# Stick breaking: the first head's weights kept, both heads' value products in one run

## The chip, the cores and the metric

The kernel runs on one core of one Trainium2 chip. The metric is the device time of one execution in microseconds (us), the median of several runs. The engines that matter here are TensorE (PE in the rows, and PEld for its weight loads), VectorE (DVE), ScalarE (ACT), GpSimd (POOL) and SyncE (SP), which issues the DMAs. Each works through its own instructions in the order in which they stand in the built program, and waits on semaphores for the others.

## The reference, cut to what matters

A trunk of two layers (512 tokens, width 1024). Each layer runs five attention branches with four heads of 64 dimensions from one projection, gates and merges them, and projects back. The change lies in the stick-breaking branch:

```
z = einsum('bqhd,bshd->bhqs', q_blk, k) * scale
strict = s_pos[None, :] < t[:, None]
log_keep = where(strict, log_sigmoid(-z), 0.0)
later = cumsum(log_keep, axis=3, reverse=True) - log_keep
a = where(strict, exp(log_sigmoid(z) + later), 0.0)
y = einsum('bhqs,bshd->bqhd', a, v)
```

## The kernel before, in words

One program, written with a tile layer that allocates buffers from pools, sets all semaphores, and decides the order of instructions on each engine by priority (in the main the order of the code) and by when buffers and inputs come free. Weights are streamed from HBM by SP in pieces of 128x1024 (`wraw`, L278); ACT rounds each piece to a high part (`whi`, L269), DVE subtracts to get the low part (`wlo`, L270), and PE multiplies in three terms, high by high, high by low and low by high (`pj`, all recorded at L259, the line of the helper `mm`). These `pj` products are most of the program. `weave` mixes generators in fixed ratios, so that an attention branch, whose steps wait for one another, stands between projections.

`sb_attn(pr)` (L921) does the stick breaking of head pair `pr`: heads 2pr (e=0) and 2pr+1 (e=1). It works on transposed scores: keys in blocks of 128 (j=3, 2, 1, 0) on the partitions, queries in the columns. Since only later queries see a key block, block j has 512-128j columns: 128, 256, 384 and 512. For each block `begin` puts the scores into a PSUM bank `sbz` (tags S and T) and computes softplus on ACT and DVE (`sp_t`), `store` splits it into a high and a low part (`sp`), `middle` adds the sums over later keys by products of `sp` with constant matrices (`ntri`, `nones`) and takes the exponential (`sb_a`, from the pool tag PT with four buffers), and `end` multiplies with the values: output `Yc`, 64 partitions (the lower half for e=0, the upper for e=1), weights `VC` of 64 columns, moving tile `sb_a`, both plain float32, which the trace records as two instructions for each product. The blocks are pipelined over three steps, so `end` of a block stands two blocks behind its `begin`. After the eighth `end`, L988 multiplies with the gate and splits the result. The stages are `weave((sb_attn(0), 8), ...)` at L1363 and L1367 and `weave((sb_attn(1), 8), ...)` at L1370, in both layers.

Other attention branches multiply with the values in `pv_pair` (L558, output `Y`): also 64 columns of weights, blocks of 128 columns, with the heads in turns, e=1, e=0.

Buffers of 128x512 float32 for nearly everything else come from the pool `st` with `NST` slots: stacked queries and keys of each branch, loads of small tables (`cbt`, L877) and of the compression weights (`wc`, L1077), temporaries. `fox_proj` (L1186) makes its sixteen stacked tiles while `dsa_attn` (L1042) still holds twelve of queries and keys and two of values.

Of the kernel before, what the change touches and what calls it, by code (L numbers as in the profile page):

```python
# [10 lines left out]
F32 = mybir.dt.float32  # L11
# [10 lines left out]
T = 512  # L22
# [3 lines left out]
EPS = 1e-6  # L26
NEG = -1e30
REPL = -3e38
NST = 31

IN_LAYOUT = (
    ('dsa_q', 256), ('dsa_ckv', 128), ('idx_q', 128), ('idx_k', 32), ('idx_w', 4), ('dsa_z', 256),
# [154 lines left out]
def trunk(ctx: ExitStack, tc: tile.TileContext, xt, memt, pos, wall, small, vec, ca, cb, out):  # L187
# [3 lines left out]
    def after(ins, *earlier):  # L191
        for e in earlier:
            if e is not None:
                tc.add_manual_dep(ins.ins, e.ins.name, dep_info, reason="issue order")
# [6 lines left out]
    wts = pool("wts")  # L201
    st = pool("st", bufs=NST)
    wk = pool("wk")
# [7 lines left out]
    def bank(name, tag, shape=(128, 512)):  # L211
        return ps.tile(list(shape), F32, name=name, tag=tag, bufs={"pj": 3, "S": 2, "T": 3}[tag])
# [45 lines left out]
    def mm(out_, lhsT, rhs, start, stop, **kw):  # L258
        return nc.tensor.matmul(out_, lhsT, rhs, start=start, stop=stop, **kw)  # L259
# [297 lines left out]

    def pv_pair(Y, pr, V, PTs, nblk, last):  # L558

        after_qk = recent[-1]  # L560
        for j in range(nblk):
            for e in (1, 0):
                m = mm(Y[64 * e:64 * e + 64, pr], V(e, j), PTs[e][:, 128 * j:128 * j + 128], j == 0, j == nblk - 1)
                after(m, last, after_qk)
# [3 lines left out]
    def causal(blocks, lag):  # L568

        pend = []  # L570
        for i, scores, sums, mask, V, done in blocks:
            n = 128 * (i + 1)
            st_ = {"Y": None, "last": None, "PT": []}
            for h in range(4):
# [4 lines left out]
                def finish(i=i, h=h, P=P, V=V, done=done, st_=st_):  # L579
# [6 lines left out]
                    if h == 3:  # L586
                        done(st_["Y"])

# [87 lines left out]
    def layer(l, xs, begin):  # L676
        vo = l * V_L
        lv = SimpleNamespace(begin=begin)
# [242 lines left out]
        def sb_attn(pr):  # L921
            SPW = [512, 384, 256, 256]
            if pr == 0:
                sp = big.tile([128, 6, T], F32R, name="sp", tag="xa")
                lv.SP = [[sp[:, 2 * min(j, 2) + s, 256 * (j == 3):256 * (j == 3) + SPW[j]] for s in range(2)] for j in range(4)]
                for s in range(2):
                    nc.vector.memset(f32(lv.SP[3][s][:, 0:128]), 0.0)
            SP = lv.SP
            out = {}

            def begin(e, j):

                h = 2 * pr + e
                n, w = SPW[j], T - 128 * j
                ks = slice(128 * j, 128 * j + 128)
                z = bank("sbz", "S" if j % 2 else "T")[:, :n]
                mm(z, lv.KC[h][:, ks], lv.QC[h][:, T - n:], True, False)
                mm(z, lv.KlC[h][:, ks], lv.QC[h][:, T - n:], False, False)
                mw = n - w + 128
                mm(z[:, :mw], identb, sbm[:, 256 - mw:], False, True)  # L940
                zw = z[:, n - w:]
                t = wk.tile([128, T], F32, name="sp_t", tag="P", bufs=3)[:, :w]
                nc.scalar.activation(t, zw, AF.Abs)
                lnexp(t, t, AF.Exp, scale=-1.0)
                lnexp(t, t, AF.Ln, bias=ones1)
                nc.vector.scalar_tensor_tensor(t, zw, 0.0, t, op0=OP.max, op1=OP.add)
                return e, j, z, t

            def middle(e, j, z, t):

                n = SPW[j]
                for jj in range(3, j - 1, -1):
                    for s in range(2):
                        mm(z[:, n - SPW[jj]:], ntri if jj == j else nones, SP[jj][s], False, jj == j and s == 1, skip_group_check=True)
                w = T - 128 * j
                a = wk.tile([128, T], F32, name="sb_a", tag="PT", bufs=4)[:, :w]
                lnexp(a, z[:, n - w:], AF.Exp)
                return e, j, a

            def store(e, j, z, t):  # L960
                shi, slo = (x[:, SPW[j] - (T - 128 * j):] for x in SP[j])
                nc.vector.tensor_copy(shi, t)
                nc.vector.tensor_sub(slo, t, f32(shi))

            def end(e, j, a):
                h = 2 * pr + e
                if not out:
                    out["Y"] = bank("Yc", "T")
                mm(out["Y"][64 * e:64 * e + 64, 128 * j:], lv.VC[:, j, 64 * h:64 * h + 64], a, j == 3, j == 0, skip_group_check=True)

            one = two = None
            for e in range(2):
                for j in (3, 2, 1, 0):
                    new = begin(e, j)
                    nxt = middle(*one) if one else None
                    store(*new)
                    if two:
                        end(*two)
                    one, two = new, nxt
                    yield  # L980
            if two:
                end(*two)
            end(*middle(*one))
            Y = out["Y"]
            if pr == 0:
                lv.YC = y_tiles()
            y = slot("yC")
            nc.vector.tensor_mul(y, Y, lv.ZC[0][:, pr])  # L988
            split(y, lv.YC[0][:, pr], lv.YC[1][:, pr])
# [424 lines left out]
```

## Time and profile before

| | |
|---|---|
| runs | 1373.56, 1374.56, 5024.1 us, median 1374.56 |
| profiled execution | 1373.34 us; span from the first to the last instruction 1371.6 us |
| PE busy | 1340.4 us, 98% of the span |
| DVE busy | 894.6 us, 65% |
| ACT busy | 691.2 us, 50% |
| DMA | 124.12 MB, mean 90 GB/s |
| mean granted TensorE clock | 0.997 |

Busy time is the union of an engine's instructions; PE's matmuls overlap their neighbours, so what one costs is read from the distance between the starts of instructions. 1.74 us of the profiled execution lie outside its span.

### The profile page before, as it was taken

To read this page: it belongs to the slowest core of one execution; us is meant where nothing else is said; L and a number is where in the kernel's file an instruction comes from. 1 tells how busy PE (TensorE), PEld (TensorE's weight loads), DVE (VectorE), ACT (ScalarE), POOL (GpSimd) and SP (SyncE) were. 2 spreads that over 40 slices of the span, in tenths; PEclk is the share of its full clock that TensorE was granted. 3 is DMA by queue.
4 is the path that set the end of the run, shared out by engine and by line. 5 is a ranking of instruction groups with operands and counts; after the bars stand their busy time and mean duration, and the time that the engine had idled before them with its cause. 6 is when DMAs were issued, how large, how long until landed. Compare 5 with 4: busy or idle time off the path is not lost. (4 is left out here: it accounts for less than half of the span.)

```text
span 1371.6 us, 19089 instructions
## 1 busy us (share of the span) xinstructions
PE 1340.4 (98%) x7240; PEld 1078.3 (79%) x7240; DVE 894.6 (65%) x1869; ACT 691.2 (50%) x1322; POOL 11.0 (1%) x28
## 2 busy tenths in 40 slices
PE   7999999999999999999999999999999999999997
PEld 6777787877788788888886777778777878887897
DVE  6877999756655444545567599995675463455454
ACT  6877825356545434434347586443574453343330
POOL 0000000000000000000000000000000000000000
PEclk9999999999999999999999999999999999999999
DMA  6441232222112222124524213212212222223231
GB/s 218 131 139 56 68 102 83 84 70 73 62 62 99 71 92 76 61 92 133 179 76 137 79 62 112 75 61 93 62 62 77 70 92 70 92 77 106 90 112 62
DMA packets 40236, 124.12 MB, mean 90 GB/s; under 512 B 4432, under 2 KB 6480, under 8 KB 40144
## 3 DMA queue, kind: packets, MB, share of 16 engines
q1 hardware_dynamic: 40144, 122.89, 27.9%
q8 instruction: 57, 0.93, 0.3%
q14 instruction: 35, 0.29, 0.1%
HBM read 118.16 MB, written 4.72 MB: 90 GB/s over the span
## 5 line engine op out<-in xcount | busy, mean ns | idle before, releaser
L259 PE MATMUL pj<-h_hi,whi 128*128 128x512 f32 x1088 | 431.9, 398 | 0.0
L259 PE MATMUL pj<-h_lo,whi 128*128 128x512 f32 x1088 | 429.2, 395 | 0.0
L259 PE MATMUL pj<-h_hi,wlo 128*128 128x512 f32 x1088 | 428.9, 394 | 0.0
L270 DVE TENSOR_TENSOR wlo<-wraw,whi 128x1024 fp32r<-128x1024 f32 x183 | 223.6, 1222 | 231.2 <-ACT whi L269 220.4
L269 ACT ACTIVATE whi<-wraw 128x1024 fp32r<-128x1024 f32 x183 | 193.6, 1059 | 353.8 <-PE pj L259 250.5
L259 PEld LDWEIGHTS pj<-h_hi,wlo 128*128 128x128 f32 x1088 | 204.6, 188 | 44.1 <-DVE wlo L270 2.2
L259 PEld LDWEIGHTS pj<-h_hi,whi 128*128 128x128 f32 x1088 | 204.7, 188 | 42.7 <-issue 4.0
L259 PEld LDWEIGHTS pj<-h_lo,whi 128*128 128x128 f32 x1088 | 204.7, 188 | 42.3 <-issue 3.8
L547 ACT ACTIVATE P<-P,nm 128x128 f32<-128x128 f32 (+3 forms) x128 | 71.5, 559 | 67.0 <-DVE nm L546 63.3
L546 DVE CUSTOM_DVE_ANT_0 P<-S,CA 128x128 f32<-128x128 f32 (+3 forms) x104 | 48.0, 469 | 40.9 <-PE S L259 40.6
L259 PE MATMUL pj<-yhi,whi 128*128 128x512 f32 (+1 forms) x192 | 72.2, 376 | 0.0
L553 PE MATMUL pt<-CA,P 128*128 128x128 f32 x384 | 69.7, 280 | 2.4 <-ACT P L1255 1.3
L259 PE MATMUL pj<-ylo,whi 128*128 128x512 f32 (+1 forms) x192 | 72.0, 375 | 0.0
L259 PE MATMUL pj<-yhi,wlo 128*128 128x512 f32 (+1 forms) x192 | 71.7, 374 | 0.0
L553 PEld LDWEIGHTS pt<-CA,P 128*128 128x128 f32 x384 | 45.1, 140 | 19.5 <-issue 7.6
L394 ACT ACTIVATE G<-pj 128x512 f32<-128x512 f32 x92 | 53.6, 583 | 0.3
L259 PE MATMUL S<-Ks,Qs 128*128 128x256 f32 (+2 forms) x160 | 50.7, 355 | 2.8 <-DVE nm L546 2.8
L893 DVE MATCH_REPLACE8 score<-m,score 128x256 f32<-128x256 f32 (+2 forms) x96 | 51.5, 539 | 0.0
L892 DVE MAX8 m<-score 128x8 f32<-128x256 f32 (+2 forms) x96 | 49.7, 545 | 0.0
L791 DVE TENSOR_TENSOR acc<-acc,G 128x512 f32<-128x512 f32 x64 | 44.0, 687 | 0.8
L790 DVE SCALAR_TENSOR_TENSOR G<-G,pj 128x512 f32<-128x512 f32 x64 | 43.6, 681 | 0.3
L259 PEld LDWEIGHTS pj<-yhi,whi 128*128 128x128 f32 x192 | 36.5, 190 | 8.3 <-issue 1.2
(478 smaller groups left out, 2053.1 us busy)
## 6 DMA issues: line engine op xcount, KB each, us to landing
wraw<-in_wall_dram SPq DMA_DIRECT2D x192, 512.0 KB, 3.7
wc<-in_wall_dram SPq DMA_DIRECT2D x16, 256.0 KB, 4.7
x<-in_xt_dram SPq DMA_DIRECT2D x8, 256.0 KB, 6.3
mraw<-in_memt_dram SPq DMA_DIRECT2D x4, 512.0 KB, 5.0
xo<-in_xt_dram SPq DMA_DIRECT2D x8, 256.0 KB, 3.7
xspill<-xn SPq DMA_DIRECT2D x8, 256.0 KB, 2.0
xo<-xspill SPq DMA_DIRECT2D x8, 256.0 KB, 2.9
out_dram<-o SPq DMA_DIRECT2D x8, 256.0 KB, 2.5
```

Source lines behind the costliest of these rows:

```text
L259: return nc.tensor.matmul(out_, lhsT, rhs, start=start, stop=stop, **kw)
L269: nc.scalar.activation(hi, raw, AF.Copy)
L270: nc.vector.tensor_sub(lo, raw, hi.bitcast(F32))
L394: i = nc.scalar.activation(*a, **k)
L546: nc.vector.tensor_tensor_reduce(P, S, mask, -1.0, 3e38, OP.add, OP.min, nm)
L547: nc.scalar.activation(P, P, AF.Exp, bias=nm, scale=-1.0, accum_out=sums)
L553: nc.tensor.transpose(pt[:, 128 * j:128 * j + 128], P[:, 128 * j:128 * j + 128], ident)
L790: nc.vector.scalar_tensor_tensor(G, G, gc, p, op0=gop, op1=OP.mult)
L791: nc.vector.tensor_add(acc, acc, G)
L892: nc.vector.max(m8, lv.work[i])
L893: nc.vector.match_replace(lv.work[i], m8, lv.work[i], REPL)
```

## The change

The value products no longer stand between the blocks. The four weight tiles of the first head are kept in a tile of their own (`held`, 128x1280, one buffer), those of the second head in the four PT buffers, and after the last `middle` the eight products go in one run over j=0 to 3, in turns e=1, e=0, chained by an order constraint. The bank for `Yc` is taken only then. To make room `NST` goes from 31 to 29. Elsewhere nothing is edited.

```
-NST = 31
+NST = 29
...
+            held = wk.tile([128, 1280], F32, name="sb_a", tag="sb_a", bufs=1)
+            first_a = [held[:, 0:512], held[:, 512:896], held[:, 896:1152], held[:, 1152:1280]]
...
-                a = wk.tile([128, T], F32, name="sb_a", tag="PT", bufs=4)[:, :w]
+                a = first_a[j] if e == 0 else wk.tile([128, T], F32, name="sb_a", tag="PT", bufs=4)[:, :w]
                 lnexp(a, z[:, n - w:], AF.Exp)
-                return e, j, a
+                out[e, j] = a
...
-            def end(e, j, a):
-                h = 2 * pr + e
-                if not out:
-                    out["Y"] = bank("Yc", "T")
-                mm(out["Y"][64 * e:64 * e + 64, 128 * j:], lv.VC[:, j, 64 * h:64 * h + 64], a, j == 3, j == 0, skip_group_check=True)
...
+            middle(*one)
+
+            Y = bank("Yc", "T")
+            last = None
+            for j in (0, 1, 2, 3):
+                for e in (1, 0):
+                    h = 2 * pr + e
+                    m = mm(Y[64 * e:64 * e + 64, 128 * j:], lv.VC[:, j, 64 * h:64 * h + 64], out[e, j], j == 0, j == 3, skip_group_check=True)
+                    after(m, last)
+                    last = m
```

**Place 1: PE, first layer, head pair 1.** Before, one product with the values stands alone between score products (`sbz`) and projections:

```order
L259 MATMUL sbz<-sp,ntri 128x256 x2
L259 MATMUL sw_p<-iq,CA 128x512
L259 MATMUL sbz<-Qs,Ks 128x384 x2
L259 LDWEIGHTS identb
L259 MATMUL sbz<-sbm,identb 128x128
L259 MATMUL pj<-h_hi,whi 128x512
L259 MATMUL Yc<-sb_a,VC 64x128
L259 MATMUL pj<-h_lo,whi 128x512
```

Now, at the end of the same pair:

```order
L259 MATMUL Yc<-sb_a,VC 64x512 x2
L259 MATMUL Yc<-sb_a,VC 64x384 x2
L259 MATMUL Yc<-sb_a,VC 64x256 x2
L259 MATMUL Yc<-sb_a,VC 64x128 x2
L553 MATMUL pt<-CA,P 128x128 x2
```

The eight single products of a pair have become one run without another instruction between them; it is the same in all four stages.

**Place 2: PE, second layer, head pair 0, first head, block j=0.** `smt_p` and `sw_p` are small products of the index branch, `sbz` those of the stick breaking. In brackets is what the instruction waits for. Before:

```order
L814 MATMUL smt_p<-CA,v_6793 128x32 x3
L259 MATMUL sbz<-Qs,Ks 128x256 [waits PE_49]
L259 MATMUL sbz<-Qs,Ks 128x256 [waits Pool_49]
L259 LDWEIGHTS identb
L259 MATMUL sbz<-sbm,identb 128x256
L259 MATMUL sbz<-sp,nones 128x256 [waits DVE_49]
L259 MATMUL sw_p<-v_6793,CA 32x512 [waits DVE_49]
L259 MATMUL sbz<-sp,nones 128x256 x3
```

Now:

```order
L814 MATMUL smt_p<-CA,v_6787 128x32 x3
L259 MATMUL sw_p<-v_6787,CA 32x512 [waits Activation_49]
L259 MATMUL sbz<-Qs,Ks 128x256 [waits PE_49]
L259 MATMUL sbz<-Qs,Ks 128x256 [waits Pool_49]
L259 LDWEIGHTS identb
L259 MATMUL sbz<-sbm,identb 128x256
L259 MATMUL sbz<-sp,nones 128x256 [waits DVE_49]
L259 MATMUL sbz<-sp,nones 128x256 x3
```

`sw_p` has moved ahead of the products that wait for DVE, and waits for ACT alone: a third bank of tag T is free, where before `sw_p` had to wait until DVE had copied `smt_p` out.

**Place 3: PE, first layer, the end of `dsa_attn`.** `S` are its scores, `pt` its transposes, `fox_e` the first product of the forgetting branch that needs the table `cbt`, behind `sel`. Before:

```order
L553 MATMUL pt<-CA,P 128x128 [waits PE_49]
L553 MATMUL pt<-CA,P 128x128 x2
L259 MATMUL S<-Ks,Qs 128x512 [waits DVE_49]
L259 MATMUL S<-Ks,Qs 128x512
L259 MATMUL fox_e<-chi,sel 128x512 [waits Activation_49]
```

Now:

```order
L553 MATMUL pt<-CA,P 128x128 [waits PE_49]
L553 MATMUL pt<-CA,P 128x128 x2
L259 MATMUL S<-Ks,Qs 128x512 [waits DVE_49]
L259 MATMUL S<-Ks,Qs 128x512
L553 MATMUL pt<-CA,P 128x128 [waits PE_49,Activation_49]
L553 MATMUL pt<-CA,P 128x128 x2
L259 MATMUL S<-Ks,Qs 128x512 [waits DVE_49]
L259 MATMUL S<-Ks,Qs 128x512
L259 MATMUL S<-Ks,Qs 128x512 [waits DVE_49]
L259 MATMUL fox_e<-chi,sel 128x512 [waits Activation_49]
```

Three more transposes and three more score products stand ahead of `fox_e`. On SP the load of `cbt` for it waited for DVE before and waits for PE now. The second layer has the same shift.

## Rows read from the trace of the kernel before

**Rows 1.** The profile page: busy time of each engine with its share of the span, and the group of the weights' high parts (busy, mean ns of one, idle time of ACT just before them and what ended it).

```profile
PE 1340.4 (98%) x7240; PEld 1078.3 (79%) x7240; DVE 894.6 (65%) x1869; ACT 691.2 (50%) x1322; POOL 11.0 (1%) x28
...
L269 ACT ACTIVATE whi<-wraw 128x1024 fp32r<-128x1024 f32 x183 | 193.6, 1059 | 353.8 <-PE pj L259 250.5
```

**Rows 2.** Busy time by stretch: bounds, length, then busy us (and instructions) of PE, PEld, DVE, ACT and POOL, granted TensorE clock, DMA share, GB/s. First the four stick-breaking stages, then parts of the stages of head pair 1.

```profile
58.00:106.00 48.00, 47.31 (x262) 35.08 (x261) 37.11 (x82) 35.88 (x75) 0.00 (x0) 1.00 0.38 121
106.00:163.00 57.00, 56.97 (x259) 41.25 (x258) 50.80 (x93) 48.20 (x90) 0.00 (x0) 1.00 0.20 64
...
727.00:772.00 45.00, 42.76 (x231) 32.87 (x230) 30.83 (x58) 29.72 (x61) 0.00 (x0) 0.96 0.37 118
772.00:836.00 64.00, 63.98 (x289) 45.86 (x288) 53.01 (x100) 49.41 (x92) 0.00 (x0) 1.00 0.19 60
...
125.00:144.00 19.00, 18.99 (x85) 13.22 (x83) 18.34 (x35) 18.29 (x39) 0.00 (x0) 1.00 0.17 55
144.00:163.00 19.00, 18.98 (x87) 13.66 (x87) 17.81 (x37) 16.28 (x29) 0.00 (x0) 1.00 0.24 79
...
793.00:813.00 20.00, 20.00 (x90) 14.19 (x89) 19.16 (x32) 17.88 (x33) 0.00 (x0) 1.00 0.16 54
813.00:836.00 23.00, 22.98 (x107) 16.44 (x106) 21.76 (x49) 20.11 (x38) 0.00 (x0) 1.00 0.18 58
```

**Rows 3.** The tile `Yc`: its instructions with minimum, median and maximum duration in ns, and what its engine waited for before them (us, times).

```profile
L259 PEld LDWEIGHTS Yc<-sb_a,VC x64: 132/136/231, 66.0 to 834.6; 128*64 128x64 f32 x64
L259 PE MATMUL Yc<-sb_a,VC x64: 272/458/902, 66.0 to 835.0; 128*64 128x128 f32 x16, 128*64 128x256 f32 x16, 128*64 128x384 f32 x16, 128*64 128x512 f32 x16
...
  ACT sb_a L388: 4.3, 13
```

**Rows 4.** The timeline of PE around a `Yc` product of 128 columns and one of 512: start, duration, instruction.

```profile
65.50 0.39 PE L259 MATMUL pj<-h_hi,wlo 128*128 128x512 f32 x1
65.73 0.39 PE L259 MATMUL pj<-h_hi,whi 128*128 128x512 f32 x1
66.05 0.43 PE L259 MATMUL Yc<-sb_a,VC 128*64 128x128 f32 x2
66.41 0.50 PE L259 MATMUL pj<-h_lo,whi 128*128 128x512 f32 x1
66.75 0.28 PE L259 MATMUL sbz<-sp,nones 128*128 128x256 f32 x1
...
104.21 0.40 PE L259 MATMUL pj<-h_hi,whi 128*128 128x512 f32 x1
104.54 1.07 PE L259 MATMUL Yc<-sb_a,VC 128*64 128x512 f32 x2
105.54 0.50 PE L259 MATMUL pj<-h_lo,whi 128*128 128x512 f32 x1
105.88 0.40 PE L259 MATMUL pj<-h_hi,wlo 128*128 128x512 f32 x1
```

**Rows 5.** The timeline of PE around a run of `pv_pair` (four products of 128 columns, heads in turns), and the weight loads of such runs from the view of the tile `Y`.

```profile
163.31 0.40 PE L259 MATMUL pj<-h_hi,wlo 128*128 128x512 f32 x1
163.64 0.66 PE L259 MATMUL Y<-PT,VE 128*64 128x128 f32 x8
164.22 0.50 PE L259 MATMUL pj<-h_hi,whi 128*128 128x512 f32 x1
164.56 0.40 PE L259 MATMUL pj<-h_lo,whi 128*128 128x512 f32 x1
...
L259 PEld LDWEIGHTS Y<-PT,VE x128: 132/137/137, 163.6 to 932.8; 128*64 128x64 f32 x128
```

**Rows 6.** DVE's groups in 106 to 163 us that belong to the top-k search of the index branch (busy us, mean ns).

```profile
L892 DVE MAX8 m<-score 128x8 f32<-128x256 f32 (+2 forms) x5 | 2.5, 522 | 0.0
L893 DVE MATCH_REPLACE8 score<-m,score 128x256 f32<-128x256 f32 (+2 forms) x4 | 2.0, 506 | 0.0
```

**Rows 7.** The timeline at place 2, second layer; in brackets the engine's idle time before an instruction and what ended it.

```profile
740.47 1.06 ACT L269 ACTIVATE whi<-wraw 128x1024 fp32r<-128x1024 f32 x1 [2.86 <-DMA wraw<-in_wall_dram]
...
745.70 0.43 PE L814 MATMUL smt_p<-CA,v 32*128 32x32 f32 x4
...
747.10 0.69 DVE L946 SCALAR_TENSOR_TENSOR sp_t<-sbz,sp_t 128x512 f32<-128x512 f32 x1
...
747.85 0.38 PE L259 MATMUL sbz<-sp,nones 128*128 128x256 f32 x1 [1.15 <-DVE sp_t L946]
...
749.23 1.04 PE L259 MATMUL sw_p<-v,CA 32*32 32x512 f32 x2 [1.00 <-DVE smt L815]
...
750.20 0.97 PE L259 MATMUL sbz<-sp,nones 128*128 128x256 f32 x5
```

**Rows 8.** The timeline at place 3, first layer, and the DMA issues of `cbt` there (count, KB each, us from issue to landing).

```profile
457.33 0.33 SPq L877 DMA_DIRECT2D cbt<-in_cb_dram  x1
...
458.16 0.73 PE L259 MATMUL S<-Ks,Qs 128*128 128x512 f32 x2 [0.80 <-DVE nm L546]
...
460.19 0.61 ACT L879 ACTIVATE sel<-cbt 128x512 fp32r<-128x512 f32 x1
...
460.94 0.42 PE L259 MATMUL fox_e<-chi,sel 128*128 128x512 f32 x1
...
cbt<-in_cb_dram SPq DMA_DIRECT2D x1, 256.0 KB, 2.6
```

**Rows 9.** The profile page: DMA issues of the compression weights, count, KB each, median us to landing.

```profile
wc<-in_wall_dram SPq DMA_DIRECT2D x16, 256.0 KB, 4.7
```

More of the change, by code (lines that the diff above doesn't have):

```diff
@@ L963, in store @@
                 nc.vector.tensor_sub(slo, t, f32(shi))
-            def end(e, j, a):
-                h = 2 * pr + e
-                if not out:
-                    out["Y"] = bank("Yc", "T")
-                mm(out["Y"][64 * e:64 * e + 64, 128 * j:], lv.VC[:, j, 64 * h:64 * h + 64], a, j == 3, j == 0, skip_group_check=True)
-            one = two = None
+            one = None
             for e in range(2):
@@ L974, in sb_attn @@
                     new = begin(e, j)
-                    nxt = middle(*one) if one else None
+                    if one:
+                        middle(*one)
                     store(*new)
-                    if two:
-                        end(*two)
-                    one, two = new, nxt
+                    one = new
                     yield
[L981 to L984, printed above, removed]
+            middle(*one)
+            Y = bank("Yc", "T")
[6 more added lines that the diff above has]
+                    last = m
             if pr == 0:
```

## The prediction

> **What bounds the kernel now.** I read the page's busy shares first. PE is busy for 98% of the span, DVE for 65% and ACT for 50%, and ACT, which prepares the weights, sits idle for 250.5 us in all because PE has not yet used the last ones [rows 1]. So the supply waits for PE, and what PE saves is time saved, as long as the stage concerned stays that way. Next I read the table by stretch for the four stick-breaking stages. In three of them PE idles for less than 0.7 us; in the second layer's first stage (727 to 772 us) it idles for 2.2 us and the granted clock falls to 0.96 on the mean, which is the lower of the two levels, 1.2 instead of 2.4 GHz, for about 0.08 x 45 = 3.6 us, 1.8 us lost [rows 2]. In the stages of head pair 1 the reader should see that DVE and ACT are nearly full too: 18.34 and 18.29 of 19 us in 125 to 144 [rows 2]. There PE is not the only limit.
>
> **What a value product costs now.** A busy PE doesn't say what one instruction costs, since neighbours overlap; the distance between starts does. Plain projections of 512 columns start 0.23 us apart (65.50, 65.73). With the 128-column product of `Yc` between them, the next projection starts 0.68 after the last, and the one after it 0.34 later: 0.45 + 0.11 = 0.56 us for the visit. The same reading of the 512-column product gives 1.10 + 0.11 = 1.21 [rows 4]. The difference, 0.65 us for 384 columns, is 1.69 ns a column; what is left of the small one, 0.56 - 0.22 = 0.34 us, is a price for each visit, for going in and out, whatever its width. A head has 1280 columns in four visits: 2.17 + 4 x 0.34 = 3.53 us. There are eight heads (two layers, two pairs, two heads), and 64 records, two for each of the 32 products, confirm the count [rows 3]: 28.2 us in all.
>
> **What the run costs.** The trace has the same shape of work in turns over two halves already, in `pv_pair`: four products of 128 columns, two for each half. By the same reading the visit costs 0.91 - 0.23 + 0.34 - 0.23 = 0.79 us [rows 5]. Side by side, two halves at a time, it should be 0.34 + 2 x 0.217 = 0.77; one after another 0.34 + 4 x 0.217 = 1.21. So the halves run at the same time there, and nothing is paid for changing from pair to pair. The new run has pairs of equal width, 512, 384, 256, 128, so I cost it at 0.34 + 2.17 = 2.51 us; four runs are 10.0. **This term is -18.2 us**: 28 x 0.34 = 9.5 for the visits that fall away, 4 x 2.17 = 8.7 for the overlap. No row shows the overlap at 512 columns; the bound on the other side is no overlap (rival 1).
>
> A rule of the Trainium skill speaks against this. TensorE: Matmul & The Clock Gate, in Part 3 under "What overlaps and what doesn't", says that a weight load overlaps matmuls in flight only if it goes to another group of rows; two column halves share all their rows. By that rule the 16 loads of a run, 0.136 us each [rows 3], would stand in the open, 2.2 us a run, and the term would be -9.5. The trace disagrees at 128 columns: eight loads of 0.137 us lie within a visit of 0.79 us together with the matmuls [rows 5].
>
> **The new wait.** All eight products now stand behind the last exponential (e=1, j=0), and behind them on PE's queue stand projections. In the built order four or five projections lie between the last `ntri` product and the run, as they lay ahead of the last single product before; today all such waits for `sb_a` come to 4.3 us of idle weight loading in 13 cases, most of it under running matmuls [rows 3]. I cost it at nothing; if the cover were gone it would be one exponential, about 0.6 us by an ACT copy of the same width [rows 8], in each of four runs. The gate multiplication behind the run starts somewhat later; its result is needed by the merge in the next stage, behind other projections.
>
> **The freed bank (place 2).** In the second layer PE idles there 1.15 us for `sp_t` and 1.00 us for the copy of `smt_p` [rows 7]. The second wait is gone, since `sw_p` no longer needs that copy, and `sw_p`'s 0.97 us (749.23 to 750.20) now lie ahead of the first wait and cover part of it. But PE comes there two visits (0.56 + 0.78) earlier, while the chain up to `sp_t` is paced by loads: ACT waited 2.86 us for `wraw` [rows 7]. Idle time after: 1.15 + 1.34 - 0.97 = 1.5 instead of 2.15, **-0.6 us**, with bounds of 0 and -2.2. I leave the clock's 1.8 us in the time, as about as much waiting and small work stays in one place; without the fall the time is 1.8 lower.
>
> **What DVE can't give (pair 1).** A pair should save 18.2 / 4 = 4.6 us. In 125 to 163 DVE has 1.85 us left, and in 793 to 836 2.08 [rows 2]. If none of its work could be put off, 2.7 and 2.5 of these would come back as waits of PE. But in the first layer's stage 4.5 us of DVE's load are steps of the top-k search [rows 6], which nothing in the stage waits for. So 0 to +5.2, and I take **+1.5 us**, nearer to the end at which the search gives way.
>
> **Two slots fewer (place 3).** By my count `dsa_attn` and `fox_proj` want 14 + 16 tiles and a few tables at once, so 31 slots are already short and 29 are shorter. It shows in the built order: three score products more stand ahead of `fox_e`, with nothing to fill the waits between them. Such a step waited 0.80 us for DVE [rows 8]. The load of `cbt` can only start when a score product has freed a slot: about 458.16 + 0.73 = 458.9 instead of 457.33, then 2.6 us to land and 0.61 for `sel`, so 462.1, against 460.94 for `fox_e` today; of these 1.2 us the moved products fill most. The work moved is work that PE must do anyway. I take one and a half such steps in each layer, **+2.5 us**, bounds 0 and +5. Behind `cbt` on SP's queue stand the next `wraw` pieces, 1.5 us later than now; ACT's 250.5 us of waiting for PE are the cover [rows 1]. Outside these stages and this place PE's order is unchanged.
>
> **Sum.** -18.2 - 0.6 + 1.5 + 2.5 = -14.8. The sum is made against the profiled execution, 1373.34 us (span 1371.6 and 1.74 around it), which lies 1.2 under the median of the runs and 0.2 under the fastest: 1358.5 us.
>
> **Rivals.**
>
> *Rival 1: the halves don't run side by side at these widths*, or the weights of one half load only when the other half's product is through, 16 x 0.136 = 2.2 us a run [rows 3], the same price. Then only visits are saved: a run is 0.34 + 4.34 = 4.7, four are 18.7, the term is -9.5, and with less freed DVE is no limit: 1373.3 - 9.5 - 0.6 + 2.5 = 1365.7; 1368 with the slots at their bound. The skill's rule above would give the same. For it: wider products are read for longer, and no row shows them in turns. Against it: the 0.79 us of rows 5.
>
> *Rival 2: the stages' chain holds the freed time.* Scores, softplus, split and exponential follow one another over three engines, and pair 1 then saves only DVE's 1.85 and 2.08 us; with the slots at +5 it is 1373.3 - 18.2 - 0.6 + 5.2 + 5 = 1364.7. For it: DVE and ACT at 96% in rows 2. Against it: the search that can give way.
>
> *Rival 3: slower, through the slots.* The compression weights `wc` also sit in slots, 16 loads in eight groups, 4.7 us to land [rows 9]. If each group got its slot so late that PE waited the whole landing, that is 8 x 4.7 = 37.6 us, so 1373.3 - 18.8 + 37.6 = 1392. It decides from 18.8 us of open waiting, half of all landings. Against it: in the built order the loads and the products that need them keep their places, but for one load that goes behind a `wraw` in the second layer.
>
> That the change doesn't do what it says, the scheduler pulling the run apart, is excluded by the built order: all four runs stand whole.
>
> **How the numbers follow.** Forecast 0.65, rival 1 0.13, rival 2 0.17, rival 3 0.05. The forecast's own range with its bounds is 1373.3 - 18.2 - 2.2 - 1.8 = 1351 to 1373.3 - 18.2 + 0 + 3 + 5 = 1363, with 3 of DVE's 5.2 us (what lies beyond is rival 2); rivals 1 and 2 lie above it up to 1368. With the 1.2 us by which the runs shown differ I give 1350 to 1369; it leaves out rival 3 and the corner in which DVE, slots and missing overlap all go badly. Two per cent, about what a measurement of this kernel can tell from no change, are 27 us, so below 1347 is faster and above 1402 slower. The whole cost of the value products is 28.2, so faster needs nearly all of it or a second gain: 0.04. Slower needs more than rival 3 as priced: 0.02. The same: 0.94.
>
> **What would show it.** In the changed trace a run of `Yc` should take about 2.3 us from its first start to the next instruction, with starts of e=1 and e=0 a few ns apart; 4.5 us would be rival 1. PE's idle time in 125 to 163 should stay under 1.5 us (rival 2: 2.5 or more). At place 2 `sw_p` should follow `smt_p` with no wait, and one wait of about 1.5 us should stand before the `sp,nones` products. At place 3 PE should idle 1 to 2 us more than before in each layer. Waits of `hid` for `wc` would be rival 3. What would make me wrong is a stage whose PE order I read as unchanged but whose buffers now come later.

## The result and the profile after

The changed kernel took 1364.98 us in the median, against 1375.01 us for the kernel before in the same comparison: ratio 0.9921, 95% interval 0.9891 to 0.995. A second comparison (the first experiment below) gave 0.9921 again, 0.9907 to 0.9934. One execution of each kernel, 5024.1 and 5879.41 us, stands in the medians and not in the ratio. So the change is worth about 11 us (9 to 13 by the second interval): clear of the noise, the same by the bound of 2%, and 4 us less gain than the 14.8 that I forecast. The profiled execution took 1365.35 us with a span of 1363.5, 8.0 us less than the profiled one of before.

The page of after, busy time of each engine; it answers to [rows 1]:

```profile
PE 1328.1 (97%) x7240; PEld 1077.0 (79%) x7240; DVE 893.5 (66%) x1869; ACT 689.6 (51%) x1322; POOL 11.2 (1%) x28
```

PE's busy time fell by 12.3 us and the span by only 8.1. So some of what was saved has become waiting. The busy times by stretch, in the columns and places of [rows 2]:

```profile
58.00:106.00 48.00, 46.17 (x274) 37.55 (x274) 39.08 (x84) 37.18 (x78) 0.00 (x0) 1.00 0.37 120
106.00:163.00 57.00, 55.98 (x272) 42.03 (x271) 52.10 (x98) 48.01 (x91) 0.00 (x0) 1.00 0.23 74
...
727.00:772.00 45.00, 41.94 (x247) 33.80 (x247) 31.04 (x59) 29.23 (x58) 0.00 (x0) 1.00 0.39 122
772.00:836.00 64.00, 62.31 (x309) 47.13 (x306) 57.29 (x105) 52.76 (x99) 0.00 (x0) 1.00 0.21 66
```

PE now idles 1.83, 1.02, 3.06 and 1.69 us in the four stages, against 0.69, 0.03, 2.24 and 0.02 before [rows 2]: 4.6 us more (the changed kernel runs ahead by up to 9 us, so that the same times hold somewhat later work). The timeline of PE around one run, first layer, pair 1:

```profile
151.37 0.39 PE L259 MATMUL pj<-h_hi,whi 128*128 128x512 f32 x1
151.69 2.38 PE L259 MATMUL Yc<-sb_a,VC 128*64 128x512 f32 x16
154.00 0.44 PE L553 MATMUL pt<-CA,P 128*128 128x128 f32 x2
```

Sixteen instructions from 151.69 to the next start at 154.00, 2.31 us, 0.2 less than the 2.51 that I had costed for halves side by side. So the missing gain must lie elsewhere.

**Where it went.** Busy time hides it: the modelled ends of matmuls overlap the next start, so a wait of 0.2 or 0.4 us still lies inside busy time. I therefore take, for each of the 7239 neighbours among PE's matmuls, the distance between their starts less the first one's columns at 2.4 GHz and 13 ns (two plain projections of 512 columns start 0.227 apart). What is left is visits, waits and slow clock. For `Yc` the whole distance is counted, and what the neighbour in front of it lost. Sums in us, by stretches; their bounds are times of the kernel before, and in the other kernels the start of the same projection, found by counting the `pj` products, since fixed times would cut the kernels at different work:

| stretch | before | after | after, second profile |
|---|---|---|---|
| value products `Yc` | 26.6 | 9.6 | 9.6 |
| to 103 (with layer 0, pair 0) | 8.8 | 10.8 | 10.0 |
| 103 to 430 (layer 0, pair 1 and on) | 29.2 | 32.0 | 31.9 |
| 430 to 530 (place 3) | 6.8 | 9.0 | 9.0 |
| 530 to 724 | 6.7 | 6.8 | 6.7 |
| 724 to 772 (layer 1, pair 0) | 6.0 | 5.7 | 4.2 |
| 772 to 1100 (layer 1, pair 1 and on) | 28.9 | 31.8 | 31.8 |
| 1100 to 1190 (place 3) | 7.1 | 7.0 | 7.1 |
| rest | 10.7 | 10.7 | 10.7 |
| sum | 130.7 | 123.4 | 121.0 |

The value products save 17.0 us. Of this 2.8 and 3.0 us are lost again in and behind the two pair-1 stages, where PE had idled for 0.03 and 0.02 us (inside the stages alone, 106 to 163 and 772 to 836, the sums go from 3.3 to 5.3 and from 3.6 to 5.9); 2.2 at the first layer's place 3; and 2.0 or 1.2 up to 103 us, of which 1.0 and 1.1 lie in the stage of pair 0 and the rest in the start-up, which moves by 1 us from run to run. The waits that the profile names for PE from 106 to 166 us and from 772 to 850 us (releaser, sum, count, longest; the view lists only those that show as idle time):

```profile
PE pt L553 <- ACT P L1257: 0.5, 1, 0.5
PE pj L259 <- DVE rt L433: 0.4, 1, 0.4
PE S L259 <- ACT sb_a L388: 0.3, 1, 0.3
PE S L259 <- ACT R L849: 0.2, 1, 0.2
...
PE pt L553 <- ACT P L1257: 0.7, 1, 0.7
PE pj L259 <- DVE rt L433: 0.4, 1, 0.4
...
PE sbz L259 <- DVE sp_t L949: 0.2, 1, 0.2
```

There is no one big wait. Many short ones, for either engine and for every branch of the stage (the stick breaking's `sp_t` and `sb_a`, the index scores' `R`, the memory attention's `P`, the rotation `rt`), have come where the single products had stood. By distances the largest in the first layer are 0.63 and 0.67 (`P`, `PT`), 0.56 (`rt`), 0.45 (`sb_a`), 0.35 and 0.29 us.

### The profile page after: what moved, and what is told of

Its sections match the earlier page's. It is cut to its first block, busy times and chain, and to the rows that moved or that the text cites. A ratio compares the mean times of both kernels' runs of the same rounds, so it can differ in the third digit from the quotient of the medians.

```text
span 1363.5 us, 19090 instructions
## 1 busy us (share of the span) xinstructions
PE 1328.1 (97%) x7240; PEld 1077.0 (79%) x7240; DVE 893.5 (66%) x1869; ACT 689.6 (51%) x1322; POOL 11.2 (1%) x28
## 4 chain that ended last, share of the span: by engine, by line
PE 71%; ACT 7%; DVE 3%; issue 2%; DMA 1%; POOLq 0%; DVEq 0%; ACTq 0%
PE pj L259 58%; PE Y L259 4%; PE pt L553 3%; PE S L259 3%; ACT whi L269 2%; ACT sw L430 1%; ACT sw L431 1%; DMA mraw<-in_memt_dram 1%; PE hr L612 1%; PE sbz L259 1%; PE hid L259 1%; ACT P L547 0%; DVE wlo L270 0%; PE ssq L259 0%; ACT sp_t L388 0%
## 5 line engine op out<-in xcount | busy, mean ns | idle before, releaser
L539 DVE COPY PT<-pt 128x512 f32<-128x512 f32 (+3 forms) x72 | 36.5, 507 | 15.3 <-PE pt L553 15.1
```

The costliest lines, as they stand in the source:

```text
L539: nc.vector.tensor_copy(o, i)
```

## Experiments

Excess, here, is the sum of the table above over 103 to 430 us and over 772 to 1100 us: 29.2 and 28.9 before, 32.0 and 31.8 after. My theory was that VectorE's load holds pair 1 (rival 2 of the prediction), and that the two slots cost the rest.

**The changed kernel again.** No edit.

> The changed kernel once more, for a tighter ratio on the chip of the other runs of this call. 1364 to 1366 us if the kernel before stands at 1374, ratio 0.992 to 0.994. If the clock falls at other places this time (none in the second layer's first stage, one at the end of the index attention, in the first profile), single runs differ by 1.7 us.

1363.19 us (1362.32 to 1363.93) against 1374.1, ratio 0.9921 [0.9907, 0.9934]; excess 31.9 and 31.8. The gain and its losses come back alike in another profile, the fall of the clock at place 3 too; only the start-up and the waits of the second layer's pair 0 move (10.8 and 10.0, 5.7 and 4.2 in the table).

**Two slots fewer, alone.**

```
-NST = 31
+NST = 29
```

> The kernel before with NST 29 in place of 31 and nothing else. Theory (two slots fewer cost time at the end of dsa_attn, where the first layer lost 2.1 us between the traces of before and after): about 2 us slower than before, 1 to 4, with the loss at fox_e in the first layer and less in the second. Rival (the slots cost nothing, the loss there comes from the run's other shifts): the time of before within 0.5 us.

1374.93 us, ratio 1.0009 [1.0, 1.0018]: 0 to 2.5 us. At place 3 of the first layer the sum of the table goes from 6.8 to 7.7, at the second's it stays (7.1 and 7.0). The slots alone cost 0.9 us there; in the changed kernel 2.2, because of the clock. PE by stretch there, the columns of [rows 2], before, with the slots alone and after:

```profile
456.00:458.00 2.00, 0.95 (x5) 0.42 (x5) 2.00 (x5) 0.84 (x3) 0.00 (x0) 1.00 0.70 221
458.00:460.00 2.00, 1.45 (x14) 0.93 (x14) 1.99 (x7) 1.59 (x5) 0.00 (x0) 1.00 0.47 131
```

```profile
456.00:458.00 2.00, 0.79 (x6) 0.34 (x4) 2.00 (x7) 1.16 (x4) 0.00 (x0) 1.00 0.69 229
458.00:460.00 2.00, 0.89 (x6) 0.46 (x8) 1.75 (x4) 1.74 (x5) 0.00 (x0) 1.00 0.13 14
```

```profile
452.00:454.00 2.00, 0.80 (x5) 0.52 (x5) 2.00 (x7) 1.16 (x4) 0.00 (x0) 1.00 0.56 188
454.00:456.00 2.00, 0.89 (x6) 0.45 (x7) 1.76 (x4) 1.56 (x5) 0.00 (x0) 0.82 0.14 25
456.00:458.00 2.00, 2.00 (x16) 1.67 (x13) 0.75 (x4) 1.82 (x5) 0.00 (x0) 0.50 0.33 115
458.00:460.00 2.00, 2.00 (x10) 1.22 (x9) 1.66 (x5) 0.51 (x2) 0.00 (x0) 0.83 0.00 0
```

In the first two stretches of each, PE idles 1.60 us before, 2.32 with the slots alone and 2.31 after: a wait of `Y` for `PT` of ScalarE has grown from 0.39 to 1.11 us, as these lines of before and after show.

```profile
459.28 0.88 PE L259 MATMUL Y<-PT,VA 128*64 128x128 f32 x12 [0.39 <-ACT PT L537]
```

```profile
455.64 1.55 PE L259 MATMUL Y<-PT,VA 128*64 128x128 f32 x12 [1.11 <-ACT PT L537]
```

Only in the changed kernel did the granted clock then fall to the lower level, 1.2 GHz, for 0.18 x 2 + 0.50 x 2 + 0.17 x 2 = 1.7 us of full speed lost. The second profile of the changed kernel shows the same there (0.55 and 0.59 from 456 to 460 us).

**The two heads one after the other.** The run stays, the turns go.

```
-            for j in (0, 1, 2, 3):
-                for e in (1, 0):
+            for e in (1, 0):
+                for j in (0, 1, 2, 3):
```

> The run of after with the two heads one after another (e=1 for all blocks, then e=0), so that the column halves don't meet. A run should take 4.4 to 4.5 us from its first start instead of 2.30. If PE sets the time everywhere, 4 x 2.15 = 8.6 us slower than after, about 1373. If DVE sets the time of the pair 1 stages (theory), the two runs there are partly covered while DVE catches up: 4.5 to 7 us slower than after, 1369 to 1372. If the overlap is worth nothing: the time of after.

1369.77 us, ratio 0.9973 [0.996, 0.9985], some 7 us slower than the changed kernel by the ratios (0.9973 - 0.9921 = 0.0052). PE around the run:

```profile
153.16 3.93 PE L259 MATMUL Yc<-sb_a,VC 128*64 128x512 f32 x16
157.02 0.44 PE L553 MATMUL pt<-CA,P 128*128 128x128 f32 x2
```

A run takes 3.86 instead of 2.31 us: the turns are worth 1.55 us a run, 6.2 in all (I had said 8.7). The run without turns is not wholly without overlap: by the starts in the trace, the second head's 512-column product starts 6 ns behind the first record of the first head's 256-column one, ahead of three records that stand before it in the code. By the distances in the same run this saves an estimated 0.6 us a run, which is the difference. Of the 6.2 us the excess gives back 0.5 and 0.7 (31.5 and 31.1): where a run takes longer, the other waits of the stage shrink. That fits the theory of waits that PE runs into, without saying what they wait for.

**The weights packed, no slot given up.** The first head's three narrower tiles go into the unused columns of the second head's tiles, its widest into a G buffer.

```
-NST = 29
+NST = 31
...
+                if e == 0 and j == 0:
+                    return wk.tile([128, T], F32, name="sb_a", tag="G", bufs=3)
+                k = j if e == 0 else (4 - j) % 4
...
+                return shared[k][:, T - w:] if e == 0 else shared[k][:, :w]
```

> The run of after, but the first head's weights lie in the unused columns of the second head's PT tiles, and the widest in a G tile, so that NST stays at 31. Theory: the 2 us of the first layer's fox_e place come back, the rest of after stays: about 1362 to 1363 where after gives 1364 to 1365. Rival (slots cost nothing): the time of after within 0.5 us.

1369.28 us, ratio 0.9968 [0.9956, 0.9981], 6 us worse than expected. Place 3 is as before the change (6.8 and 7.0), but pair 1 lost more, 36.0 and 34.4: the gate projection there waited for the G buffer that was held, and the clock fell behind it.

```profile
139.14 0.79 PE L259 MATMUL pj<-h_hi,whi 128*128 128x512 f32 x1 [1.74 <-DVE Z L423]
```

and the stretch around it:

```profile
138.00:142.00 4.00, 2.86 (x8) 2.38 (x9) 4.00 (x16) 2.89 (x8) 0.00 (x0) 0.65 0.28 92
```

**Packed, the widest tile on its own, 30 slots.**

```
-                    return wk.tile([128, T], F32, name="sb_a", tag="G", bufs=3)
+                    return wk.tile([128, T], F32, name="sb_a", tag="sb_a", bufs=1)
```

> The packed kernel again (the first head's three narrower weight tiles in the unused columns of the second head's tiles), but with the widest in a tile of its own of 2 KB a partition, and 30 slots in place of 31. Theory, what the packed kernel lost was the third G buffer alone: the 1.7 us wait of the gate projection and its clock fall go, 3 to 5 us, and half of the slots' price comes back, 0.5 to 1: 1364 to 1366, as fast as the changed kernel or 1 us faster. Rival, shared tiles themselves delay the second head's exponentials: still 1368 to 1370.

1366.27 us, ratio 0.9942 [0.9929, 0.9954]. The G wait is gone (excess 32.1 and 31.6, as after), so it was that buffer; but both places 3 now show a clock fall and sums of 9.3 and 9.5 us. One slot fewer is no cheaper than two.

**Packed, the widest tile on its own, 31 slots.**

```
-            hs = sm.tile([64, 128], F32, name="ht", bufs=1)
+            hs = sm.tile([128, 128], F32, name="ht", tag="ht", bufs=1)[0:64]
...
-                kb = sm.tile([128, 4, 32], F32, name=f"kcb{pr}", bufs=1)
+                kb = sm.tile([128, 4, 32], F32, name=f"kcb{pr}", tag="kcb1" if pr else "ht", bufs=1)
```

> The packed kernel with 31 slots, as before the change, and the widest tile of the first head in a tile of its own of 2 KB; the 0.5 KB missing for it come from two small tiles of the compression (ht and kcb0), which now share one buffer. Theory, what the changed kernel pays for its two slots is the wait and the clock fall at the end of the index attention in the first layer, about 2 us, and the G buffer was all that the first packed kernel lost: ratio to the kernel before 0.990 to 0.991, 1360.5 to 1362 where the changed kernel stands at 1363 to 1365. Rival, waits and clock falls only change their places: 0.992 or above.

1362.01 us (1361.42 to 1362.97), ratio 0.9914 [0.99, 0.9927], the best by its median of the versions that leave nothing out, though its interval overlaps the changed kernel's. Place 3 is back at 6.9 and 7.0, with the clock full there; the last two lines are the second layer's stage of pair 0:

```profile
454.00:456.00 2.00, 1.87 (x18) 1.50 (x19) 1.74 (x8) 1.65 (x5) 0.00 (x0) 1.00 0.19 68
456.00:458.00 2.00, 2.00 (x15) 1.82 (x15) 1.48 (x5) 1.85 (x5) 0.00 (x0) 1.00 0.00 0
...
740.00:744.00 4.00, 3.10 (x14) 1.99 (x15) 3.82 (x6) 3.88 (x9) 0.00 (x0) 0.82 0.48 166
744.00:748.00 4.00, 4.00 (x25) 3.81 (x25) 3.81 (x7) 1.40 (x3) 0.00 (x0) 0.75 0.17 35
```

So the price of the slots at place 3 is shown and avoided there; pair 1's is not (31.8 and 31.6). In the time it doesn't show clear of the noise: the clock now falls in the second layer's stage of pair 0, where the changed kernel shows no fall in either profile and all nine edited versions of it show one. The expectation's rival, that falls of the clock only change their places, is not excluded.

**The changed kernel with less for VectorE.** Left out: the additions of the index scores of heads 1 to 3.

```
-                        nc.vector.scalar_tensor_tensor(a[i], R, lv.wI[:, i, h:h + 1], a[i], op0=OP.mult, op1=OP.add)
```

> The kernel after without the additions of the index scores of heads 1 to 3 (nine operations on DVE in each layer, 5.3 us, all in the pair 1 stage), so the selection is computed from the first index head alone; PE and ACT do the same work. Theory (DVE sets the time of the pair 1 stage in after): PE's waits there go, 1.5 to 2.7 us a layer, so 3 to 5 us faster than after, 1360 to 1362. Rival (the waits are the latency of the chain of scores, softplus and split, not DVE's load): within 1 us of after.

1361.45 us, ratio 0.991 [0.9896, 0.9923]: against the 1364.98 of the first comparison this looks like the theory's 3 us; against the second run of the changed kernel it doesn't, since the intervals overlap. The excess is 32.1 and 30.5: nothing in the first layer, 1.2 us less in the second. Inside the two stages alone it is 0.9 and 1.1 less (4.4 and 4.8), but in the first layer that comes back behind the stage. VectorE was as full as before in 115 to 140 us (third busy column, of this kernel and of after):

```profile
115.00:140.00 25.00, 24.66 (x117) 19.30 (x116) 24.46 (x51) 23.13 (x47) 0.00 (x0) 1.00 0.13 43
```

```profile
115.00:140.00 25.00, 24.65 (x113) 18.73 (x112) 24.25 (x43) 22.36 (x44) 0.00 (x0) 1.00 0.18 57
```

Fifty-one instructions stand where 43 stood: the order is decided anew and other work moves up.

**The same in the kernel before.**

> The kernel before without the additions of the index scores of heads 1 to 3 (9 VectorE instructions and 5.3 us of VectorE in each layer's stage of head pair 1; the index scores are those of the first head alone). Theory, VectorE became a limit only with the change: TensorE idles 0.03 us in that stage before, so nothing is gained, 0 to 1 us, 1372.5 to 1374. Rival, VectorE held time there already: 3 us or more faster, as the changed kernel was without the same additions.

1381.52 us, ratio 1.0052 [1.0038, 1.0065], 7 us slower with less to do, which neither the theory nor the rival had. Up to 156 us nothing had changed (0.2 us); the new order then lost 3 us behind the stage in the first layer and 4 in the second, in waits such as this one of PE for the compression weights (the longest from 160 to 203 us):

```profile
PE hid L259 <- DMA wc<-in_wall_dram: 1.0, 1, 1.0
```

It says that this stage of before had no room to gain, and that work taken away is not a clean test here.

**Half of the Qi work on GpSimd.**

```
+                    else:
+                        nc.gpsimd.tensor_copy(Qi[c:c + 32], qr[r])
+                        nc.gpsimd.tensor_sub(Qi[c + 32:c + 64], qr[r], f32(qhi[r]))
```

> The changed kernel with half of the copies and subtractions that make Qi (L839 and L840, 4 of 8 each in a layer, 2.5 us of ScalarE and 2.7 us of VectorE) on GpSimd, which is idle there. The output is the same. Theory, VectorE and ScalarE together hold the stage of head pair 1: both get 2.5 us of room in each layer, and 1.5 to 2.5 us of it show in each layer, 1360 to 1362 where the changed kernel stands at 1365. If only VectorE held it, the gain shows in the second layer alone, as without the additions, 1.5 to 2.5 in all. Rival, GpSimd takes far longer for a slice than the two engines (no row shows such an operation on it), so the score products of each head wait for it: as the changed kernel, or 1 to 6 us slower.

1370.84 us, ratio 0.998 [0.9971, 0.9989], 8 us slower than the changed kernel. While GpSimd works, VectorE's own subtractions take about twice as long in the first layer (1.5 times in the second). The groups of Qi's subtractions in the first layer's stage, of after and of this kernel:

```profile
L840 DVE TENSOR_TENSOR Qi<-rt,qhi 32x512 fp32r<-32x512 f32 x8 | 5.5, 684 | 0.2
```

```profile
L841 DVE TENSOR_TENSOR Qi<-rt,qhi 32x512 fp32r<-32x512 f32 x4 | 5.4, 1346 | 0.1
...
L844 POOL TENSOR_TENSOR Qi<-rt,qhi 32x512 fp32r<-32x512 f32 x4 | 6.1, 1517 | 0.3
```

Four subtractions cost VectorE 5.4 us where eight had cost 5.5 (4.1 in the second layer): little or no room was made, so this doesn't test the theory either.

**The top-k search kept out of pair 1.**

```
-                nc.vector.tensor_sub(slo, t, f32(shi))
+                lv.stored = nc.vector.tensor_sub(slo, t, f32(shi))
...
-                    nc.vector.max(m8, lv.work[i])
+                    after(nc.vector.max(m8, lv.work[i]), lv.stored if r == 0 else None)
```

> The changed kernel with the first search step of each block row (L892) ordered behind the last split of head pair 1, so that no step of the top-k search stands in the stage of head pair 1. Theory, VectorE's load holds the first layer's stage, and 4 to 5 us of it are search steps: PE idles 1 us less there and the stage keeps 1 to 2 us more; the search then ends later, behind the memory attention, where it may cost as much again. 1362 to 1365, with the gain seen between 125 and 163 us of the first layer. Rival, ScalarE holds the stage (it is as full): no change between 125 and 163 us.

1366.61 us, ratio 0.9949 [0.9935, 0.9963], some 4 us slower than the changed kernel. The first search step of the changed kernel starts only at 140.07 us, so the edit tests no more than the last 18 us of the stage. There, in the changed kernel, a rotation step that PE waits for stands behind search steps:

```profile
155.17 0.41 DVE L893 MATCH_REPLACE8 score<-m,score 128x256 f32<-128x256 f32 x1
...
155.50 0.68 DVE L433 TENSOR_TENSOR rt<-pj,cosQ 128x512 f32<-128x512 f32 x1
...
156.23 0.50 PE L259 MATMUL pj<-h_hi,whi 128*128 128x512 f32 x1 [0.40 <-DVE rt L433]
```

With the search later that wait is gone, but `pt` waits 1.2 us for `P` of ScalarE where it had waited 0.5. Between the same projections the first layer's stage (106 to 163 us of before) loses 5.5 us against 5.3, and the excess is 32.3 and 33.0. A wait taken away at VectorE came back at ScalarE.

**Both engines relieved, by half of the index products.**

```
-                for c in (0, 64):
+                for c in (0,):
...
-                    mm(S, Qi[:, 128 * i:128 * i + 128], Ki[:, 0:n], True, True)
+                    mm(S, Qi[0:64, 128 * i:128 * i + 128], Ki[0:64, 0:n], True, True)
```

> The changed kernel with the index scores over 64 rows in place of 128, which leaves out the products with the low part of the keys (Ki's second half), and so the copies and subtractions that make the second half of Qi: 2.5 us of ScalarE and 2.7 us of VectorE less in each layer's stage of head pair 1, nothing put in their place; PE's work there stays, since it goes by columns. Theory, VectorE and ScalarE together hold the stage: 1.5 to 2.5 us in each layer, 1360 to 1362. Rival, the chain from score to exponential holds it, whatever the load: 1363 to 1365.

1376.74 us, ratio 1.0014 [1.0005, 1.0023]: 13 us slower than the changed kernel. My premise that PE's work stays was wrong. A product over 64 rows between projections over 128:

```profile
126.65 0.39 PE L259 MATMUL pj<-h_hi,wlo 128*128 128x512 f32 x1
126.97 0.38 PE L259 MATMUL S<-Ki,Qi 64*128 64x256 f32 x1
127.28 0.50 PE L259 MATMUL pj<-h_hi,whi 128*128 128x512 f32 x1
127.71 0.44 PE L259 MATMUL S<-Ki,Qi 64*128 64x384 f32 x1
```

The product of 256 columns takes 0.31 us to the next start, where its columns at 2.4 GHz are 0.107: 0.2 us for coming out. The projection in front of it takes 0.32 instead of 0.23, 0.1 for going in, and the one between the two products 0.43, 0.2. The other products of this kind show the same, save those that follow one another. PE also waits 2.49 us for `P` at 157.46 us, as in the next experiment. Inconclusive for the theory.

**Both engines relieved, with products of full height.** The relu and the addition of heads 1 to 3 are left out.

```
-                        nc.scalar.activation(R, S, AF.Relu)
-                        nc.vector.scalar_tensor_tensor(a[i], R, lv.wI[:, i, h:h + 1], a[i], op0=OP.mult, op1=OP.add)
```

> The changed kernel without both the relu (L849, ScalarE, 9 in a layer, 4.2 us) and the addition (L850, VectorE, 5.3 us) of the index scores of heads 1 to 3; the score products themselves stay, so PE's work is the same and in products of the same shape, but nothing is waited for behind them. Theory, VectorE and ScalarE together hold the stage of head pair 1, so that taking load from one alone moves the wait to the other: with both relieved 2 to 3 us of the lost 4 come back in each layer, 1357 to 1360. Rival, PE's order and the chains behind it hold it (the order is planned again once the work is gone): as without the additions alone, 1361 to 1364.

1369.5 us, ratio 0.9962 [0.9949, 0.9976], some 6 us slower than the changed kernel, excess 34.0 and 34.8. The busy times in 150 to 160 us (VectorE and ScalarE are the third and fourth busy column), and behind the wait of the second layer that is shown below:

```profile
150.00:160.00 10.00, 7.52 (x37) 5.86 (x37) 9.96 (x22) 7.50 (x14) 0.00 (x0) 1.00 0.41 126
...
825.00:829.00 4.00, 4.00 (x15) 3.47 (x14) 3.96 (x9) 1.82 (x4) 0.00 (x0) 0.57 0.88 269
```

and the longest wait of PE in the stage:

```profile
PE S L259 <- ACT P L1253: 2.5, 1, 2.5
```

ScalarE has room now, VectorE is as full as ever, since other work has moved up, and PE waits 2.5 us at one score product of the memory attention. The timeline of the same wait in the second layer (in brackets the idle time before an instruction):

```profile
821.29 1.06 ACT L269 ACTIVATE whi<-wraw 128x1024 fp32r<-128x1024 f32 x1
...
821.59 0.28 PE L259 MATMUL S<-KlE,Qs 128*128 128x256 f32 x1
...
822.38 0.59 ACT L431 ACTIVATE sw<-pj 32x512 f32<-32x512 f32 x1
...
822.99 0.72 ACT L388 ACTIVATE sp_t<-sp_t,ones 128x512 f32<-128x512 f32 x1
823.73 0.47 ACT L1253 ACTIVATE P<-S,nm 128x256 f32<-128x256 f32 x1
...
824.35 0.38 PE L259 MATMUL S<-KE,Qs 128*128 128x256 f32 x1 [2.48 <-ACT P L1253]
```

The exponential `P` stands on ScalarE behind a weight piece, a rotation and a logarithm, 2.4 us of other work, and in the new order nothing stands on PE between its last score product and the next one. In the second layer the clock falls behind this wait (0.57 of full speed from 825 to 829 us, 1.7 us lost), in the first it doesn't. With 9.5 us less work for the two engines in each layer the stage loses more, so the sum of their work alone does not set its length; how the work stands in the queues counts as well.

## Why the prediction was right in the time and wrong in the sum

The time lay in the range, at the rival's number rather than the forecast's: 1364.98 us against 1358.5 and, for rival 2, 1364.7. That it meets rival 2 within 0.3 us is luck: that sum held 5 us for the slots, which cost 2.2, and nothing for the first layer's pair 0, nor for the start-up of the profile.

**The run (-18.2): nearly right, -17.0.** A run starts its halves 6 to 7 ns apart and takes 2.31 us (2.40 with what its neighbours lose; I had 2.51). The value products of before were the smaller ones: 26.6 us by distances instead of 28.2, 3.3 a head, as the mean over all their places, where I had read two visits among projections. Rival 1 is dead: sixteen loads of 0.137 us, 2.2 us in all, lie within the 2.31 us of the run together with its matmuls, and with the turns taken away the run takes 3.86. The rule from the Trainium skill that I had set against this (TensorE: Matmul & The Clock Gate, Part 3, "What overlaps and what doesn't": a weight load overlaps matmuls in flight only in another group of rows) does not describe these two column halves, at 512 columns no more than at 128.

**The new wait on the exponential (0): right.** Before the run shown above a projection starts 0.32 us ahead, 0.1 more than its columns want.

**Place 2 (-0.6): right in the mechanism, incomplete in the stage.** In the second layer of after:

```profile
743.36 0.43 PE L814 MATMUL smt_p<-CA,v 32*128 32x32 f32 x4
...
743.73 1.04 PE L259 MATMUL sw_p<-v,CA 32*32 32x512 f32 x2
...
746.50 1.10 PE L259 MATMUL sbz<-sp,nones 128*128 128x256 f32 x6 [1.18 <-DVE sp_t L949]
```

`sw_p` follows without a wait and one wait of 1.18 is left where 1.15 and 1.00 stood [rows 7], and the clock stays at 1.00 through the stage, where it had cost 1.7 us. But in the first profile PE, early, also waits for splits at other blocks of the pair (0.49 and 0.36 us at 736 and 737 us); in the second it doesn't. The stage's sum is 5.7 and 4.2 against 6.0: -0.3 and -1.7, and without the clock +1.4 and 0. So what the stage gained came from the clock, which I had left in the time, and no more from the waits.

**DVE's limit in pair 1 (+1.5): the step that failed.** It measured +5.8 (2.8 and 3.0; 2.7 and 2.9 in the second profile), beyond the bound of 5.2; 4.3 of it lies inside the two stages, the rest behind them. Three things were wrong in it. I sized it by VectorE's free time alone; ScalarE, which I had read as nearly full in the same rows, ends as many of the waits. I took the top-k search for slack; with the search out of the way, the first layer's stage lost as much (5.5 against 5.3 us). And I let the price be at most what an engine lacks over the stage, while the waits come one by one. My reading, which no run shows, is that they come wherever a chain of score, softplus or exponential is longer than the products left in front of it, and that the single value products, 0.6 to 1.2 us each, had been that filler. My own sign for it failed too: PE's idle time in 125 to 163 us is 0.9 us, which I had put down as the forecast's side, since waits this short lie inside busy time.

What stays open is whether load or the length of the chains holds the stage. The excess of pair 1 was the same in every kernel in which the single products are gone and nothing else is (31.8 to 32.1 and 31.6 to 31.8), and fell by 0.5 and 0.7 with a longer run. With less for VectorE it fell by 1.2 in the second layer alone (by 0.9 and 1.1 inside the stages, which speaks for load); with less for VectorE and ScalarE it rose. But each edit of the load also changed PE's order, so none held the order fixed. An order held by hand with the load removed was not tried.

**Two slots (+2.5): right in size, +2.2** (2.1 in the second profile), alone 0.9. The mechanism was in part another: not one and a half uncovered waits in each layer, but in the first layer only 0.7 us more of idle time and the fall of the clock behind it. Packing the tiles, with 31 slots, took it away.

**What the sum left out:** pair 0 of the first layer, whose waits I took as unchanged. Its sum rose by 1.0 and 1.1 us, by short waits that I had priced at nothing: in 58 to 103 us

```profile
PE pj L259 <- DVE wlo L270: 0.8, 2, 0.5
...
PE sbz L259 <- ACT sb_a L388: 0.4, 1, 0.4
```

Rival 3 did not happen: `hid` waits for no `wc` in the changed kernel; it did in the kernel before with less for VectorE, 1.0 us.

## What to carry to other kernels

Price a product that leaves a full stage twice: by its own distance between starts, and by the cover that it may have given to the chains around it; here, where two other engines were 96% busy in part of the stage, 5.8 of the some 8.5 us that pair 1 saved (half of 17.0, an estimate) came back as many short waits. Look for such waits in the distances between PE's starts, not in its idle time, and cut the kernels to be compared at the same work, not at the same time. A run that needs more memory should first look for unused columns in tiles that live anyway; giving up slots cost 2.2 of the 17.0 us, and borrowing a buffer that the stage itself uses cost more. Taking work away to test a limit tells little where a scheduler decides the order again.

## What the runs showed of the hardware

- Plain float32 products over two column halves run side by side also at 512, 384 and 256 columns: 16 instructions in 2.31 us in turns, 3.86 one head after the other, where the halves still met once.
- A product over 64 rows of contraction between products over 128 costs 0.1 us on the way in (0.2 where a single projection stands between two of them) and 0.2 on the way out, beside its columns. The Trainium skill says that changing the tiling mode drains TensorE (TensorEngine Tiling (Array Packing), "Key Properties"); it gives no price, and whether this one is that drain no run here separates.
- With GpSimd at work a VectorE subtraction of two SBUF inputs took 1.346 us on the mean in the first layer and 1.014 in the second, instead of 0.684. The Trainium skill has the rule (SBUF — State Buffer, "SBUF: two separate sides": VectorE with two SBUF inputs and a GpSimd operation that reads SBUF exclude each other on a shared pair of ports); the trace agrees.
- 2.31 us of idle time within 4 us at place 3 were followed by the lower clock in the changed kernel (1.7 us lost, in both its profiles), and 2.32 us at the same place with the slots alone were not.
